# A list scheduler's costs and the pieces of a transposed softmax, in a hybrid decoder layer on one core

## The chip, the cores and the metric

The kernel runs on one core of a Trainium2 chip. The metric is device time in microseconds (us) of one execution. A core has five engines with queues of their own: TensorE (PE in the profile; its weight loads are PEld), VectorE (DVE), ScalarE (ACT), GpSimd (POOL) and SyncE (SP), which issues nearly all DMA transfers here. Each engine runs its instructions in the order of the program; semaphores hold an instruction until what it depends on is done. SBUF is the working memory, PSUM the one that matmuls write, in banks of 512 float32 values for each of 128 partitions.

## What is computed

One layer with 512 tokens and a model width of 1,024. A wide input projection feeds four causal mixers of width 512, each is gated, projected and merged, and an output projection is added to the input:

```python
xn = rms_norm(x, norm_g); z = xn @ w_in              # (512, 10528) columns, split
y_a = fox_attention(rms_norm(qa), rms_norm(ka), va, fa + b_forget)   # A: 8 heads
y_b = rg_lru(xb, ...)                                # B: recurrence
y_c = nsa_attention(rms_norm(qc), ...)               # C: 8 heads, three attentions
y_d = spatial_gating(ud, vd, ...)                    # D: gated MLP
ys = [y_a * silu(ga), y_b * silu(gb), y_c * silu(gc), y_d * silu(gd)]
proj = einsum('bsnw,nwd->bsnd', ys, w_branch)
out = x + sum_n(sigmoid(mg_n) * proj_n) @ w_out
```

What matters for the change is the causal softmax attention over 512 keys: once for each of the 8 heads of A, and twice for each of the 8 heads of C (called `s` and `w` in the kernel), so 24 times:

```python
s = q_i @ k.T * scale + bias                         # block i of 128 queries
p = masked_softmax(s, pos_k <= t)                    # rows are queries
o = p @ v                                            # needs p with keys on partitions
```

## The kernel before

**Precision.** Each float32 operand is split into a high part (a copy rounded to the matmul's type) and a low part (the difference): a copy on ACT or POOL, then a subtraction on DVE. A dense product takes three matmuls, high by high, high by low and low by high, each of 128 x 128 weights by 512 columns.

**Attention.** `scores` computes the four blocks of 128 queries of one unit (a head of A, or `s` or `w` of a head of C): two matmuls a block into a bank of pool `s`, mask and maximum on DVE, exponential on ACT into `p`, and normalisation on POOL. Because the mask is causal, `p` holds ten blocks of 128 x 128. `finish` transposes them on TensorE into PSUM (`transposes`, L734), so that keys lie on partitions: ACT copies the high part `ph` out and DVE subtracts it to make the low part `pl`. `values` multiplies both by the values into bank `o`. The ten blocks form three groups (keys 0; keys 1 and 3; keys 2), as `GROUPS` lists. They are transposed in five pieces of two blocks (`PIECES`), each into half a bank: `thalf` (L270) deals out the halves in turn. While A runs there is one such bank, `tb0`; for C there is a second, `tb1`, and `thalf` alternates between the two banks before it takes their other halves. Both have `tb` as their name in the profile.

**Filler.** Between these steps `fill(gap)` advances a queue of dense projections (`z_kv`, `z_qc`, `z_vd`, `z_ga`, `z_gd`, `z_ud`, `z_xb`, `z_gc` and others), so that TensorE has matmuls while it waits for the softmax.

**Order.** From the first projection to the end of attention the program doesn't issue directly: `Order` records each operation and, when a stack of pools is closed (`settle`), plans all that is pending. `plan` is a list scheduler. It keeps for each engine a time at which it is free, takes the engine that can start first, and of its operations that are ready the one that was recorded first. `cost` gives two numbers per operation: how long the engine is taken and when the result is there. `WAKE` is added between a result and an operation of another engine that needs it: 0.036 us for ACT, 0.033 for DVE, 0.064 for SP, 0.2 for POOL and 1.2 for PE. What the planner assumes sets the order only; on the chip, semaphores hold what isn't ready. Its tables know nothing of two engines that hinder each other. Behind attention, from the branches' merge on, the program issues in the order in which it is written.

**The start of C.** After the last head of A, DVE computes reciprocal roots (`tsc`), POOL multiplies keys and queries by them (`zkm`, `zq_c`), TensorE transposes these (`kt_s`, `qt_c`), ACT and DVE make operands of them (`ka_s`, `kb_s`, `q_c`), and the scores `s_s` follow. `sl` is a chain of small operations on DVE for branch B, `w_gd` and `w_w1k` are weights being split, `th_ga` and `y_a` belong to A's gate, `tblk` and `tblv` to C's compressed keys and values.

Of the kernel before, what the change touches and what calls it, by code (L numbers as in the profile page):

```python
# [11 lines left out]
F32R = mybir.dt.float32r  # L12
# [50 lines left out]
def f32(ap):  # L63
    return ap.bitcast(F32)


class Order:


    WAKE = {"ACT": 0.036, "DVE": 0.033, "SP": 0.064, "POOL": 0.2, "PE": 1.2}  # L70

    def __init__(self, nc):
        self.eng = {"ACT": nc.scalar, "DVE": nc.vector, "POOL": nc.gpsimd, "PE": nc.tensor, "SP": nc.sync}
        self.on, self.ops, self.seen, self.ring, self.before, self.stacks = False, [], {}, {}, {}, {}
        self.free = dict.fromkeys(self.eng, 0.0)
        self.wire, self.end, self.pending, self.queued = 0.0, {}, [], None

    def pool(self, real, stack):
        p = _Pool(self, real)
        self.stacks.setdefault(id(stack), []).append(p)  # L80
        return p

# [13 lines left out]
    def add(self, name, method, args, kw):  # L96
        aps = [(n == 0, a) for n, a in enumerate(args)] + [(k in ("out", "accum_out"), a) for k, a in kw.items()]
        aps = [(w, a) for w, a in aps if isinstance(a, bass.AP)]
        n, need = len(self.ops), {}
        boxes = [(w, *self.area(a)) for w, a in aps]  # L100
        for w, t, *box in boxes:
            if w and t in self.before:
                need.update((m, True) for m, *_ in self.seen.get(self.before[t], ()))
            for m, w2, b in self.seen.get(t, ()):
                if (w or w2) and box[0] < b[1] and b[0] < box[1] and box[2] < b[3] and b[2] < box[3]:
                    need[m] = need.get(m, False) or not (name == "PE" == self.ops[m][0] and w and w2)
        if self.queued is not None and self.ops[self.queued][0] == name:
# [3 lines left out]
        self.ops.append((name, method, args, kw, need, self.cost(name, kw, aps), {b[1] for b in boxes}))  # L111
        self.pending.append(n)
        return n

    @staticmethod
    def cost(name, kw, aps):

        free = max(a.free_size() for _, a in aps)
        scalar = any(not w and x.free_size() == 1 for w, x in aps)
        if name == "PE":  # L120
# [12 lines left out]
    def plan(self):  # L133

        ops, left, then, ready = self.ops, {}, {}, {}
        soon, able = {e: [] for e in self.eng}, {e: [] for e in self.eng}
        free, wire, end, out = dict(self.free), self.wire, self.end, []
        for i in self.pending:
            name, need = ops[i][0], ops[i][4]
            ready[i], left[i] = 0.0, 0  # L140
            for m, whole in need.items():
                if m in end:
                    ready[i] = max(ready[i], end[m] + self.WAKE[name] if whole else 0.0)
# [5 lines left out]
        done = {}  # L149
        for _ in self.pending:  # L150
            best = None
            for e in self.eng:
                t = free[e]
# [15 lines left out]
            out.append((i, t, free[e], wire, done[i]))  # L169
            for j in then.get(i, ()):  # L170
                f = ops[j][0]
                ready[j] = max(ready[j], done[i] + self.WAKE[f] if ops[j][4][i] else t)
# [5 lines left out]
    def settle(self, stack=None):  # L178
# [7 lines left out]
        for i, t, free, wire, done in out:  # L186
            name, method, args, kw, *_ = self.ops[i]
            getattr(self.eng[name], method)(*args, **kw)  # L188
            self.free[name], self.wire, self.end[i] = free, wire, done
        gone = {o[0] for o in out}  # L190
        self.pending = [i for i in self.pending if i not in gone]

# [10 lines left out]


class _Pool:
    def __init__(self, order, real):
        self.order, self.real, self.names, self.lines = order, real, [], {}

    def tile(self, *args, tag=None, bufs=None, **kw):
        if tag is not None:  # L210
            kw.update(tag=tag, bufs=bufs)
        t = self.real.tile(*args, **kw)
        self.names.append(t.tensor.name)
        if tag is not None:
            line = self.lines.setdefault(tag, [])
            if len(line) >= bufs:
# [6 lines left out]
def tile_hybrid_layer(ctx: ExitStack, tc: tile.TileContext, x, xT, units, small, bsp, out):  # L223
# [484 lines left out]
    def scores(u, gap):  # L708
# [25 lines left out]
    def transposes(u, n):  # L734
# [22 lines left out]
    def finish(u, gaps):  # L757
# [14 lines left out]
        fill(gaps[3])  # L772
# [969 lines left out]
```

## Time and profile before

| | before |
|---|---|
| median of 3 runs | 725.02 us (724.39 to 725.21) |
| the profiled execution, its own time | 724.89 us |
| its span, first to last instruction | 723.2 us |
| instructions in it | 9,672 |
| TensorE's granted clock, mean | 0.997 |
| bytes read from HBM, written | 65.64 MB, 2.10 MB |

The profile's page gives each engine's busy time, the span in 40 slices, the DMA queues, the chain of work that ended last, and the costliest groups of instructions. Its busy time of TensorE counts a matmul until its modelled end, so that two matmuls in a row overlap in it. DMA is light behind the first slices; its busy share in tenths, slice by slice:

```
DMA  8613222112112521200011223235432242143302
```

In the rows of the waits, an engine's idle time is put down to what ended it: engine, tile, "<-", engine and tile that released it, then the total in us, how many times, and the longest. In rows of the timeline the first number is the start in us from the span's start, the second the duration.

### The profile page before, as it was taken

Reading aid. Unit: us, or ns where it says so; the run is one execution under the profiler, and the core shown is the slowest. Engines: PE = TensorE matmul, PEld = TensorE weight load, DVE = VectorE, ACT = ScalarE, POOL = GpSimd, SP = SyncE. Lnnn points to the kernel's source line nnn. Section 1 sums busy time; section 2 is a strip of 40 time slices with the busy share of each in tenths; the row PEclk is TensorE's granted clock in tenths of the full one; section 3 lists DMA queues with packets and bytes.
Section 4 is the critical chain, followed back from the end, with each engine's and each line's share of the span. In section 5 each row is a group of like instructions: output and inputs, shape, how many; then the busy total and the mean of one; then the engine's idle time right before and its main releaser. Section 6 shows DMA issues by size and latency. Waiting matters only on the chain.

```text
span 723.2 us, 9672 instructions
## 1 busy us (share of the span) xinstructions
PE 703.2 (97%) x3357; PEld 574.4 (79%) x3357; DVE 575.8 (80%) x1138; ACT 367.2 (51%) x725; POOL 167.7 (23%) x230
## 2 busy tenths in 40 slices
PE   8999999999998999989999999999999999999997
PEld 6888788777866888878887787888888888888876
DVE  6797866666489838888997979999868858958995
ACT  4452565664523336766665891434443551554641
POOL 4115552442445312323343322100000000000000
PEclk9999999999999999999999999999999999999999
DMA  8613222112112521200011223235432242143302
GB/s 321 239 43 116 76 89 70 59 59 76 42 59 88 175 90 57 88 30 30 30 59 43 76 87 102 88 109 182 145 118 88 85 138 98 36 139 117 116 30 87
DMA packets 20640, 68.35 MB, mean 95 GB/s; under 512 B 2416, under 2 KB 2800, under 8 KB 20592
## 3 DMA queue, kind: packets, MB, share of 16 engines
q1 hardware_dynamic: 20160, 67.25, 27.9%
q8 instruction: 26, 0.43, 0.2%
q10 hardware_dynamic: 432, 0.49, 0.2%
q14 instruction: 22, 0.18, 0.1%
HBM read 65.64 MB, written 2.10 MB: 94 GB/s over the span
## 4 chain that ended last, share of the span: by engine, by line
PE 75%; DVE 14%; ACT 8%; issue 2%; DMA 1%; POOL 0%; DVEq 0%; SPq 0%; ACTq 0%
PE pj L201 10%; PE tb L188 4%; PE z_ud L188 3%; PE z_qc L188 3%; PE z_ka L188 3%; PE z_gb L201 3%; PE z_qa L188 3%; PE z_va L188 3%; PE z_mg L201 3%; PE z_xb L188 3%; PE mg2y L201 2%; PE z_kv L188 2%; PE z_vd L188 2%; PE mg3y L201 2%; PE mg1y L201 2%; PE z_gd L188 2%
## 5 line engine op out<-in xcount | busy, mean ns | idle before, releaser
L201 PE MATMUL pj<-w_wb,yh 128*128 128x512 f32 x256 | 80.2, 390 | 0.0
L201 PEld LDWEIGHTS pj<-w_wb,yh 128*128 128x128 f32 x256 | 48.1, 188 | 10.4 <-ACT tm L201 0.4
L201 PE MATMUL pj<-w_wb,yl 128*128 128x512 f32 x128 | 49.8, 389 | 0.0
L188 DVE TENSOR_TENSOR pl_a<-tb,ph_a 128x256 fp32r<-128x256 f32 x40 | 16.1, 421 | 18.7 <-PE tb L188 8.0
L201 DVE TENSOR_TENSOR w_wb<-r_wb,w_wb 128x512 fp32r<-128x512 f32 x32 | 21.8, 713 | 9.5 <-ACT w_wb L201 8.5
L201 PEld LDWEIGHTS pj<-w_wb,yl 128*128 128x128 f32 x128 | 24.0, 188 | 4.9
L188 ACT CAST ph_a<-tb 128x256 fp32r<-128x256 f32 x40 | 14.2, 375 | 25.6 <-PE tb L188 21.9
L188 ACT ACTIVATE p_s<-p_s,nm_s 128x512 f32<-128x512 f32 (+3 forms) x32 | 17.9, 562 | 12.9 <-DVE nm_s L188 12.7
L188 PE MATMUL z_gd<-xh,w_gd 128*128 128x512 f32 x64 | 23.6, 415 | 0.5 <-DVE sgd L188 0.5
L188 POOL TENSOR_SCALAR p_w<-p_w,nm_w 128x128 f32<-128x128 f32 (+3 forms) x32 | 16.9, 546 | 27.1 <-DVE nm_w L188 27.1
L188 POOL TENSOR_SCALAR p_s<-p_s,nm_s 128x128 f32<-128x128 f32 (+3 forms) x32 | 17.2, 556 | 25.3 <-ACT ph_w L188 10.8
L188 DVE CUSTOM_DVE_ANT_0 p_a<-s_a,maskm 128x512 f32<-128x512 f32 (+3 forms) x32 | 15.5, 488 | 9.3 <-PE s_a L188 8.1
L188 PE MATMUL z_xb<-xh,w_xb 128*128 128x512 f32 x64 | 22.9, 415 | 0.0
L188 PE MATMUL z_ud<-xh,w_ud 128*128 128x512 f32 x64 | 22.7, 402 | 0.0
L188 ACT ACTIVATE p_a<-p_a,nm_a 128x512 f32<-128x512 f32 (+3 forms) x32 | 17.9, 561 | 9.4 <-DVE nm_a L188 9.1
L188 PE MATMUL z_ga<-xh,w_ga 128*128 128x512 f32 x64 | 22.0, 404 | 0.0
L188 POOL TENSOR_SCALAR p_a<-p_a,nm_a 128x128 f32<-128x128 f32 (+3 forms) x32 | 18.6, 598 | 14.8 <-DVE nm_a L188 14.8
L188 ACT ACTIVATE p_w<-p_w,nm_w 128x512 f32<-128x512 f32 (+3 forms) x32 | 18.0, 564 | 7.3 <-DVE nm_w L188 6.2
L201 PE MATMUL z_gb<-xh,w_gb 128*128 128x512 f32 x64 | 21.1, 391 | 0.0
L201 ACT CAST w_wb<-r_wb 128x1024 fp32r<-128x1024 f32 x12 | 12.6, 1048 | 15.5 <-issue 15.5
L188 DVE TENSOR_TENSOR pl_s<-tb,ph_s 128x256 fp32r<-128x256 f32 x40 | 16.0, 415 | 4.9 <-ACT ph_s L188 4.6
L188 ACT CAST ph_w<-tb 128x256 fp32r<-128x256 f32 x40 | 13.9, 369 | 11.3 <-PE tb L188 8.9
(812 smaller groups left out, 2336.1 us busy)
## 6 DMA issues: line engine op xcount, KB each, us to landing
r_wb<-in_units_dram SPq DMA_DIRECT2D x16, 512.0 KB, 3.8
xt<-in_x_dram SPq DMA_DIRECT2D x4, 512.0 KB, 8.8
r_ga<-in_units_dram SPq DMA_DIRECT2D x4, 512.0 KB, 3.6
r_gd<-in_units_dram SPq DMA_DIRECT2D x4, 512.0 KB, 3.8
r_ud<-in_units_dram SPq DMA_DIRECT2D x4, 512.0 KB, 4.4
r_gc<-in_units_dram SPq DMA_DIRECT2D x4, 512.0 KB, 3.7
r_xb<-in_units_dram SPq DMA_DIRECT2D x4, 512.0 KB, 3.6
r_gb<-in_units_dram SPq DMA_DIRECT2D x4, 512.0 KB, 3.6
```

The source lines that it names most:

```text
L188: getattr(self.eng[name], method)(*args, **kw)
L201: return lambda *args, **kw: real(*args, **kw).ins
```

## The change

**Pieces.** The ten blocks are transposed in three pieces, one for each group, of four, four and two blocks; a piece has a bank to itself, and the banks are dealt out in turn. `transposes` issues four (or two) transposes, one copy on ACT and one subtraction on DVE of 512 (or 256) columns. `finish` calls the three pieces with `fill` and `values` between them in another order.

**The planner.** Its costs are new for every engine. A matmul now has a weight load that runs ahead of it and a time for its columns. PE's allowance of 1.2 us becomes 0.05 in `WAKE` plus 0.5 in `MARGIN` for results of other engines; POOL's becomes 0.11. Two exclusions are new. An operation that touches a PSUM tile is put off until the engine that touched that tile last is done with it, if that was another engine (`bank`). And operations of DVE (with a wide operand that isn't in PSUM) and of POOL that are marked so don't overlap: the later one starts when the other is done (`shared`).

```diff
-    WAKE = {"ACT": 0.036, "DVE": 0.033, "SP": 0.064, "POOL": 0.2, "PE": 1.2}
+    WAKE = {"ACT": 0.036, "DVE": 0.033, "SP": 0.064, "POOL": 0.11, "PE": 0.05}
+    MARGIN = {"ACT": 0.0, "DVE": 0.0, "SP": 0.0, "POOL": 0.0, "PE": 0.5}
...
         if name == "PE":
-            return max(0.112, free / 2400 + 0.018), free / 2400 + 0.175
+            weights = kw["lhsT"] if "lhsT" in kw else wide[0]
+            return aps[0][1].free_size() / 2400, 0.112 * max(64, min(128, weights.free_size())) / 128
         if name == "SP":
-            return 0.37, aps[0][1].partition_size() * free * 4 / 330e3
+            return 0.37, aps[0][1].partition_size() * aps[0][1].free_size() * 4 / 350e3
         if name == "DVE":
-            t, over = 0.17 + free / 850 + 0.06 * scalar, 0.08
-        elif name == "ACT":
-            t, over = 0.15 + free / 1140 + 0.09 * scalar + 0.12 * ("accum_out" in kw), 0.09
-        else:
-            two = sum(not w and x.free_size() == free for w, x in aps) > 1
-            t, over = (0.3 + free / 430 if two else 0.2 + free / 1100 + 0.1 * scalar), 0.02
-        return t - over, t
+            alone = bool(wide) and method not in ("tensor_reduce", "reciprocal", "memset") and not any(
+                x.tensor.name in self.psum for x in wide)
+            return 0.155 + free / 960 + 0.05 * scalar + 0.06 * (method == "tensor_tensor_scan" and free / 100), alone
+        if name == "ACT":
+            return 0.15 + free / 1140 + 0.09 * scalar + 0.15 * ("accum_out" in kw), False
+        if method == "memset":
+            return 0.1 + free / 1200, False
+        return (0.09 + free / 540 if len(wide) > 1 and method == "tensor_tensor" else 0.18 + free / 1170), True
...
             i = heapq.heappop(able[e])
-            busy, whole = ops[i][5]
-            free[e] = t + busy
-            if e == "SP":
-                wire = max(wire, t + 1.6) + whole
-                done[i] = wire + 0.6
+            open_ = max((bank[x][1] + self.WAKE[e] for x in ops[i][7] if x in bank and bank[x][0] != e), default=0.0)
+            if open_ > t:
+                heapq.heappush(soon[e], (open_, i))
+                continue
+            a, b = ops[i][5]
+            if e == "PE":
+                start = max(t + b, load)
+                load, free[e], done[i] = start + a + 0.014, start + max(a - 0.098, 0.003), start + a + 0.172
+            elif e == "SP":
+                wire = max(wire, t + 1.3) + b
+                free[e], done[i] = t + a, wire + 0.86
             else:
-                done[i] = t + whole
+                done[i] = t + a
+                if b:
+                    if shared[1] != e and shared[0] > t + 0.06:
+                        done[i] = shared[0] - 0.06 + a
+                    shared = done[i], e
+                free[e] = done[i] - self.OVER[e]
+            for x in ops[i][7]:
+                bank[x] = e, done[i]
...
-    PIECES = ((0, ((0, 0), (0, 1))), (0, ((0, 2), (0, 3))), (1, ((1, 1), (1, 2))), (1, ((1, 3), (3, 3))),
-              (2, ((2, 2), (2, 3))))
+    PIECES = (((0, 0), (0, 1), (0, 2), (0, 3)), ((1, 1), (1, 2), (1, 3), (3, 3)), ((2, 2), (2, 3)))
...
-        g_, blocks = PIECES[n]
-        t_ = thalf()
-        for c, (j, i) in enumerate(blocks):
+        ps_["ti"] = (ps_["ti"] + 1) % len(ps_["tb"])
+        n = P * len(PIECES[g_])
+        t_ = ps_["tb"][ps_["ti"]][:, 0:n]
+        for c, (j, i) in enumerate(PIECES[g_]):
             PE.transpose(t_[:, c * P:(c + 1) * P], u.p[:, OFF[i] + j * P:OFF[i] + (j + 1) * P], identf)
...
-        ACT.copy(ph[:, c:c + 256], t_)
-        DVE.tensor_tensor(pl_[:, c:c + 256], t_, f32(ph[:, c:c + 256]), op=ALU.subtract)
+        ACT.copy(ph[:, 0:n], t_)
+        DVE.tensor_tensor(pl_[:, 0:n], t_, f32(ph[:, 0:n]), op=ALU.subtract)
...
         transposes(u, 0)
+        fill(gaps[0])
         transposes(u, 1)
-        fill(gaps[0])
+        values(u, o, 0)
+        fill(gaps[1])
         transposes(u, 2)
-        values(u, o, 0)
-        transposes(u, 3)
-        fill(gaps[1])
-        transposes(u, 4)
         fill(gaps[2])
         values(u, o, 1)
```

The planner's answer moves instructions on every engine. Two places show how.

**TensorE, in the second head of A** (unit `a1`, tile `p_a_762`): `tb_79` is the bank `tb0`, `z_qc` are dense matmuls, `o_a` the values. Before, with four transposes nine matmuls ahead of the first row:

```order
L188 MATMUL o_a_800<-ph_a_801,v_a 128x512
L188 MATMUL tb_79<-identf,p_a_762 128x128 x2
L188 MATMUL z_qc_791<-w_qc.01_797,xh 128x512
L188 MATMUL o_a_800<-pl_a_802,v_a 128x512
L188 MATMUL tb_79<-identf,p_a_762 128x128 x2
L188 MATMUL z_qc_791<-w_qc.01_797,xl 128x512
L188 MATMUL z_qc_791<-w_qc.01_797,xh 128x512 x2
L188 MATMUL z_qc_791<-w_qc.01_797,xl 128x512
L188 MATMUL z_qc_791<-w_qc.01_797,xh 128x512
L188 MATMUL z_qc_792<-w_qc.01_797,xh 128x512
L188 MATMUL z_qc_792<-w_qc.01_797,xl 128x512
L188 MATMUL tb_79<-identf,p_a_762 128x128 x2
```

and now, at the same place:

```order
L211 MATMUL tb_79<-identf,p_a_762 128x128 x4
L211 MATMUL o_a_800<-pl_a_802,v_a 128x512
L211 MATMUL z_qc_791<-w_qc.01_797,xh 128x512
L211 MATMUL z_qc_791<-w_qc.01_797,xl 128x512
L211 MATMUL z_qc_791<-w_qc.01_797,xh 128x512 x2
L211 MATMUL z_qc_791<-w_qc.01_797,xl 128x512
L211 MATMUL z_qc_791<-w_qc.01_797,xh 128x512
L211 MATMUL o_a_800<-ph_a_803,v_a 128x384
L211 MATMUL z_qc_792<-w_qc.01_797,xh 128x512
L211 MATMUL z_qc_792<-w_qc.01_797,xl 128x512
L211 MATMUL tb_79<-identf,p_a_762 128x128 x2
```

Two matmuls stood between the second and the third visit to the bank, and seven between the third and the last; now there is one visit less, and ten matmuls stand between the last two.

**DVE, at the start of C**: before, from the second `sl` operation behind the split of `w_w1k` to the operand `kb_s`, behind which `q_c` follows at once:

```order
L188 TENSOR_SCALAR sl<-sl 128x4
L188 TENSOR_TENSOR sl<-sl 128x4
L188 TENSOR_SCALAR sl<-sl 128x4
L188 RECIPROCAL sl<-sl 128x4
L188 TENSOR_TENSOR sl<-sl 128x4 x2
L188 TENSOR_SCALAR sl<-sl 128x4
L188 SCALAR_TENSOR_TENSOR sl<-sl 128x4 x2
L188 SCALAR_TENSOR_TENSOR th_ga_1984<-th_ga_1984,z_ga_1971 128x512
L188 SCALAR_TENSOR_TENSOR sl<-sl 128x4
L188 TENSOR_TENSOR y_a<-y_a,th_ga_1984 128x512
L188 TENSOR_TENSOR w_gd_1994<-r_gd_1993,w_gd_1994 128x512
L188 SCALAR_TENSOR_TENSOR kb_s<-kt_s,cc,ka_s 64x512 x2
```

and now, from the split of `w_w1k` on:

```order
L211 TENSOR_TENSOR w_w1k_1950<-r_w1k_1949,w_w1k_1950 128x1024
L211 SCALAR_TENSOR_TENSOR th_ga_1952<-th_ga_1952,z_ga_1939 128x512
L211 TENSOR_TENSOR sl<-sl 128x4
L211 TENSOR_TENSOR y_a<-y_a,th_ga_1952 128x512
L211 TENSOR_TENSOR w_gd_1962<-r_gd_1961,w_gd_1962 128x512 x2
L211 SCALAR_TENSOR_TENSOR kb_s<-kt_s,cc,ka_s 64x512 x2
L211 SCALAR_TENSOR_TENSOR q_c_1936<-qt_c_1935,cc,q_c_1936 64x512 x2
```

All but one of the `sl` operations stand behind the scores now, and one half of `w_gd` more stands ahead of `kb_s`.

More of the change, by code (lines that the diff above doesn't have):

```diff
@@ L75, in __init__, with pool @@
         self.free = dict.fromkeys(self.eng, 0.0)
-        self.wire, self.end, self.pending, self.queued = 0.0, {}, [], None
-    def pool(self, real, stack):
-        p = _Pool(self, real)
+        self.wire, self.shared, self.load, self.psum, self.bank = 0.0, (0.0, None), 0.0, set(), {}
+        self.end, self.pending, self.queued = {}, [], None
+    def pool(self, real, stack, psum):
+        p = _Pool(self, real, psum)
         self.stacks.setdefault(id(stack), []).append(p)
@@ L110, in add, with cost @@
             self.seen.setdefault(t, []).append((n, w, box))
-        self.ops.append((name, method, args, kw, need, self.cost(name, kw, aps), {b[1] for b in boxes}))
+        self.ops.append((name, method, args, kw, need, self.cost(name, method, kw, aps), {b[1] for b in boxes},
+                         {b[1] for b in boxes} & self.psum))
         self.pending.append(n)
         return n
-    @staticmethod
-    def cost(name, kw, aps):
+    def cost(self, name, method, kw, aps):
         free = max(a.free_size() for _, a in aps)
         scalar = any(not w and x.free_size() == 1 for w, x in aps)
+        wide = [x for w, x in aps if not w and x.free_size() > 1]
         if name == "PE":
-            return max(0.112, free / 2400 + 0.018), free / 2400 + 0.175
+            weights = kw["lhsT"] if "lhsT" in kw else wide[0]
+            return aps[0][1].free_size() / 2400, 0.112 * max(64, min(128, weights.free_size())) / 128
         if name == "SP":
-            return 0.37, aps[0][1].partition_size() * free * 4 / 330e3
+            return 0.37, aps[0][1].partition_size() * aps[0][1].free_size() * 4 / 350e3
         if name == "DVE":
-            t, over = 0.17 + free / 850 + 0.06 * scalar, 0.08
-        elif name == "ACT":
-            t, over = 0.15 + free / 1140 + 0.09 * scalar + 0.12 * ("accum_out" in kw), 0.09
-        else:
-            two = sum(not w and x.free_size() == free for w, x in aps) > 1
-            t, over = (0.3 + free / 430 if two else 0.2 + free / 1100 + 0.1 * scalar), 0.02
-        return t - over, t
+            alone = bool(wide) and method not in ("tensor_reduce", "reciprocal", "memset") and not any(
[6 more added lines that the diff above has]
+        return (0.09 + free / 540 if len(wide) > 1 and method == "tensor_tensor" else 0.18 + free / 1170), True
+    OVER = {"ACT": 0.098, "DVE": 0.082, "POOL": 0.028}
     def plan(self):
@@ L136, in plan @@
         soon, able = {e: [] for e in self.eng}, {e: [] for e in self.eng}
-        free, wire, end, out = dict(self.free), self.wire, self.end, []
+        free, end, out = dict(self.free), self.end, []
+        wire, shared, load, bank = self.wire, self.shared, self.load, dict(self.bank)
+        margin = lambda e, m: self.WAKE[e] + (self.MARGIN[e] if ops[m][0] not in (e, "SP") else 0.0)
         for i in self.pending:
@@ L142, in plan @@
                 if m in end:
-                    ready[i] = max(ready[i], end[m] + self.WAKE[name] if whole else 0.0)
+                    ready[i] = max(ready[i], end[m] + margin(name, m) if whole else 0.0)
                 else:
@@ L148, in plan @@
                 heapq.heappush(soon[name], (ready[i], i))
-        done = {}
-        for _ in self.pending:
+        done, todo = {}, len(self.pending)
+        while len(out) < todo:
             best = None
@@ L161, in plan @@
             i = heapq.heappop(able[e])
[L162 to L169 removed]
+            open_ = max((bank[x][1] + self.WAKE[e] for x in ops[i][7] if x in bank and bank[x][0] != e), default=0.0)
[9 more added lines that the diff above has]
+                free[e], done[i] = t + a, wire + 0.86
+            else:
+                done[i] = t + a
[6 more added lines that the diff above has]
+                bank[x] = e, done[i]
+            out.append((i, dict(free), wire, shared, load, done[i]))
             for j in then.get(i, ()):
                 f = ops[j][0]
[L172 removed]
+                ready[j] = max(ready[j], done[i] + margin(f, i) if ops[j][4][i] else t)
                 left[j] -= 1
@@ L185, in settle @@
             out = out[:max((k + 1 for k, o in enumerate(out) if self.ops[o[0]][6] & names), default=0)]
-        for i, t, free, wire, done in out:
+        for i, self.free, self.wire, self.shared, self.load, self.end[i] in out:
             name, method, args, kw, *_ = self.ops[i]
+            self.bank.update((x, (name, self.end[i])) for x in self.ops[i][7])
             getattr(self.eng[name], method)(*args, **kw)
-            self.free[name], self.wire, self.end[i] = free, wire, done
         gone = {o[0] for o in out}
@@ L213, in tile @@
         self.names.append(t.tensor.name)
+        if self.psum:
+            self.order.psum.add(t.tensor.name)
         if tag is not None:
@@ L228, in pool @@
     def pool(name, stack=ctx, **kw):
-        return order.pool(stack.enter_context(tc.tile_pool(name=name, bufs=1, reuse_waits="tile", **kw)), stack)
+        return order.pool(stack.enter_context(tc.tile_pool(name=name, bufs=1, reuse_waits="tile", **kw)), stack,
+                          kw.get("space") is PSUM)
     def behind(op):
```

14 lines of the change are left out of this document (6 added, 8 removed).

## The prediction

> **What bounds the kernel now.** The page's first part gives each engine's busy time, the fourth the chain of work that ended last; one row of that chain in order of time shows TensorE undisturbed.
>
> ```profile
> PE 703.2 (97%) x3357; PEld 574.4 (79%) x3357; DVE 575.8 (80%) x1138; ACT 367.2 (51%) x725; POOL 167.7 (23%) x230
> PE 75%; DVE 14%; ACT 8%; issue 2%; DMA 1%; POOL 0%; DVEq 0%; SPq 0%; ACTq 0%
> 523.68 5.44 PE mg2z L201 x24
> ```
>
> TensorE carries 75% of the chain, and its undisturbed pace is 5.44 / 24 = 0.227 us for a matmul of 512 columns. The change adds and removes no matmul, so it can only win or lose time in which TensorE does not issue. Busy time by stage (length, then TensorE's busy time; DVE's is the fourth number) shows where that is:
>
> ```profile
> 75.00:200.00 125.00, 121.46 (x606) 97.87 (x606) 83.13 (x186) 73.95 (x171) 51.86 (x80) 1.00 0.21 68
> 200.00:275.00 75.00, 70.18 (x332) 56.34 (x331) 56.98 (x126) 23.30 (x51) 26.68 (x29) 0.98 0.33 106
> 275.00:400.00 125.00, 120.64 (x685) 99.95 (x683) 107.96 (x328) 83.94 (x239) 45.45 (x74) 1.00 0.15 47
> 400.00:723.20 323.20, 318.07 (x1430) 261.26 (x1429) 271.23 (x398) 153.94 (x211) 17.27 (x13) 1.00 0.31 102
> ```
>
> The planner orders what lies before about 395 us: first the eight heads of branch A, then the start of branch C, then its sixteen heads. TensorE is not busy for 3.5, 4.8 and 4.4 us there, 12.7 in all. That is a lower bound, since records are longer than the pace. The waits between 75 and 400 us say for what (total, times, longest), of the weight loads first and then of the matmuls:
>
> ```profile
> PEld tb L188 <- ACT ph_a L188: 4.1, 8, 0.9
> ...
> PEld tb L188 <- DVE pl_a L188: 3.1, 5, 0.7
> PEld tb L188 <- ACT ph_s L188: 2.9, 6, 0.7
> ...
> PEld tb L188 <- DVE pl_s L188: 2.1, 3, 1.5
> PEld tb L188 <- ACT ph_w L188: 1.8, 5, 0.5
> ```
>
> ```profile
> PE s_s L188 <- DVE q_c L188: 2.9, 1, 2.9
> PE tb L188 <- DVE pl_a L188: 1.9, 4, 0.5
> PE tb L188 <- ACT ph_s L188: 1.1, 3, 0.4
> ...
> PE tb L188 <- DVE pl_s L188: 1.0, 1, 1.0
> PE tb L188 <- ACT pc L188: 0.8, 1, 0.8
> ...
> PE tb L188 <- ACT ph_a L188: 0.5, 1, 0.5
> ...
> PE tb L188 <- ACT ph_w L188: 0.4, 2, 0.2
> ```
>
> Two things stand out: the bank `tb` into which probabilities are transposed (14.0 us by the weight loads, 5.7 us by the matmuls), and one wait of 2.9 us.
>
> **Part 1, whole banks.** One head of branch A, in order of time:
>
> ```profile
> 115.98 0.38 PE L188 MATMUL tb<-identf,p_a 128*128 128x128 f32 x2
> ...
> 116.42 0.40 PE L188 MATMUL o_a<-pl_a,v_a 128*128 128x512 f32 x1
> 116.44 0.37 ACT L188 CAST ph_a<-tb 128x256 fp32r<-128x256 f32 x1 [1.72 <-PE tb L188]
> ...
> 116.86 0.14 PEld L188 LDWEIGHTS tb<-identf,p_a 128*128 128x128 f32 x1 [0.47 <-ACT ph_a L188]
> ...
> 117.23 0.42 DVE L188 TENSOR_TENSOR pl_a<-tb,ph_a 128x256 fp32r<-128x256 f32 x1 [1.72 <-PE tb L188]
> 117.71 0.14 PEld L188 LDWEIGHTS tb<-identf,p_a 128*128 128x128 f32 x1 [0.71 <-DVE pl_a L188]
> 117.71 0.33 PE L188 MATMUL tb<-identf,p_a 128*128 128x128 f32 x1 [0.52 <-DVE pl_a L188]
> ...
> 117.79 0.48 PE L188 MATMUL z_qc<-w_qc.01_797,xl 128*128 128x512 f32 x1
> ```
>
> The pair at 115.98 fills one half of the bank, the pair at 116.86 the other. Yet the second pair starts only after ACT's copy of the first half (116.81), DVE's subtraction only after that transpose, and the last transpose only after DVE (117.65): three engines take turns on one bank, whichever half they touch. A transpose takes 0.11 us (115.98 to 116.42 hold two and one matmul of `z_qc`, 0.227). So the matmul of 117.79 was due at 116.42 + 0.227 + 0.22 = 116.87: 0.92 us lost, where the weight loads' rows show 0.47 + 0.71 = 1.18. With that ratio of 0.78 the 14.0 us cost 10.9 us; the matmuls' rows give 5.7. I take 10.9, because the timeline prices it like that.
>
> What replaces it? Ordered rows times these durations give TensorE's other work between the last transpose of a piece and the first of the next in the same bank. Before, 0.45 us once in each of the eight heads of branch A, and under 1 us at some 25 of 79 places in branch C. Now 2.22 us or more at all 23 places of branch A, and in branch C 1.8 or more at 44 of 47. A full bank needs a transpose, ACT's copy of 512 columns and DVE's subtraction from PSUM; the nearest rows of that shape (minimum, median, maximum in ns) are
>
> ```profile
> L188 ACT ACTIVATE th_ga<-z_ga x4: 598/600/605, 198.4 to 219.9; 128x512 f32<-128x512 f32 x4
> L188 DVE SCALAR_TENSOR_TENSOR th_ga<-th_ga,z_ga x4: 672/678/682, 199.0 to 225.2; 128x512 f32<-128x512 f32 x4
> ```
>
> which make 0.33 + 0.60 + 0.68 and three gaps of 0.05 (116.81 to 116.86): 1.76 us, below 2.22. Before, a half needed 0.33 + 0.37 + 0.42 + 0.15 = 1.27 us, and where 1.59 us of work stood ahead of it, the head's last pair came on time, 0.23 us after the matmul ahead:
>
> ```profile
> 119.27 0.39 PE L188 MATMUL z_qc<-w_qc.01_797,xl 128*128 128x512 f32 x1
> 119.50 0.38 PE L188 MATMUL tb<-identf,p_a 128*128 128x128 f32 x2
> ```
>
> Three places of branch C stay short of 1.76, by 2.8 us together at most, and ACT or DVE will at times be at something else when the bank is handed over. I leave 0.125 us a head, 24 heads, 3.0 us (between 0 and the 10.9). **Part 1: 7.9 us less.** Five copies and five subtractions a head become three of each: 5 x 0.37 - (2 x 0.60 + 0.37) = 0.28 us less of ACT and 5 x 0.42 - (2 x 0.68 + 0.42) = 0.32 us less of DVE, 6.7 and 7.7 us over 24 heads. I count that as nothing: it lies beside TensorE's work. If DVE were the bound in branch C, up to 16 x 0.32 = 5.1 us of it would count.
>
> **Part 2, the start of branch C.** DVE, then TensorE:
>
> ```profile
> 220.95 0.57 DVE L188 TENSOR_TENSOR sl<-sl 128x4 f32<-128x4 f32 x1
> 221.55 0.98 DVE L188 TENSOR_SCALAR sl<-sl 128x4 f32<-128x4 f32 x1
> ...
> 227.18 1.51 DVE L188 SCALAR_TENSOR_TENSOR kb_s<-kt_s,cc,ka_s 64x512 fp32r<-64x512 f32 x2
> 228.72 1.53 DVE L188 SCALAR_TENSOR_TENSOR q_c<-qt_c,cc,q_c 64x512 fp32r<-64x512 f32 x2
> ```
>
> ```profile
> 226.36 0.39 PE L188 MATMUL z_gd<-xh,w_gd 128*128 128x512 f32 x1
> 229.60 0.47 PE L188 MATMUL s_s<-ka_s,q_c 128*128 128x512 f32 x1 [2.86 <-DVE q_c L188]
> ```
>
> Tiny operations on four columns, up to 0.98 us each while GpSimd works, stand ahead of `kb_s` and `q_c`, which the scores wait for. From 220.95 to 227.18 DVE spends 6.2 us; the new order keeps one `sl` (0.57), `th_ga` (0.68), `y_a` and two halves of `w_gd` (0.7 each, by the same width): 3.4 us, or about 4.7 if GpSimd stretches the last three. So the operands come 1.5 to 2.8 us sooner, and the ordered rows put 0.7 us more matmul work ahead of the scores: the wait of 229.60 - 226.36 - 0.23 = 3.0 us shrinks to 0 to 0.8; I take 0.4, a gain of 2.6. The wait has a sequel:
>
> ```profile
> 230.60:234.00 3.40, 3.40 (x11) 2.82 (x10) 3.37 (x8) 1.41 (x4) 1.04 (x1) 0.50 0.34 104
> ```
>
> For 3.4 us the granted clock is 0.50, which costs 1.7 us, and that goes with the wait. The Trainium skill, in "TensorE: Matmul & The Clock Gate", Part 1, says the clock drops after an idle window of about 3.4 us. By that rule a wait of 3.0 us would cost no clock, and the sum would be 1.7 us worse; the trace shows the drop behind this shorter wait, and the trace decides. Against it, `tblk` of 1,024 columns (estimated at 1.3 us, twice the row of 512) moves ahead of the last `tsc` step, for which GpSimd and the first transposes of this stage wait; but 1.6 us more matmuls stand ahead of these too. I charge 0.5. On the DMA queue two loads change place with the next one; the later of them,
>
> ```profile
> L188 SPq DMA_DIRECT2D r_w1v<-in_units_dram x2: 328/328/328, 231.6 to 237.1; - x2
> L188 ACT CAST w_w1v<-r_w1v x2: 1047/1048/1048, 240.3 to 255.5; 128x1024 fp32r<-128x1024 f32 x2
> ```
>
> is issued 8.7 us ahead of its first use, so one load more ahead of it costs nothing unless that lead is used up. **Part 2: 2.6 + 1.7 - 0.5 = 3.8 us less**, between 0 (GpSimd's chain holds the scores anyway) and 4.7.
>
> **Part 3, thinner margins.** The planner assumed 1.2 us between a result and a matmul that uses it, now 0.55. Work between a piece's last transpose and the first use of its copy was 1.0 us or more in 71 of 72 cases, now below that in five; a full copy needs 0.33 + 0.60 + 0.10 = 1.03. Five short by 0.2 to 0.4 make 1.5 us, late scores something more: **2.0 us lost**, between 0 and 14 (0.1 us at each of 72 `ph` and 72 `pl`).
>
> **Sum** against the profiled execution's own 724.89 us (span 723.2; the median of the runs is 725.02): 724.89 - 7.9 - 3.8 + 2.0 = **715.2 us**. Behind 400 us the same work follows, with 5.1 us not busy in 323; it starts earlier by as much.
>
> **Rivals.** (a) DVE becomes the bound in branch C: 107.96 of 125 us busy speaks for it, the 17 us idle there against. Then the part of `tb` in branch C, (2.9 + 2.1 + 1.8) x 0.78 = 5.3 us, stays: 720.5. (b) The wait of part 2 stays, because GpSimd's eight products set it: 719.0. (c) The change does not do what it says: bank waits turn into waits for `ph` and `pl`, the start stays: 724.9. (d) Slower: the thin margin costs 0.1 us at each of the 144 first uses, 14.4 instead of 2.0: 727.6; it decides from 11.7 / 144 = 0.08 us. Against it stands that the distances for `pl` mostly exceed 1.76. (e) All goes: `tb` 14.0, start 4.7, no loss: 706.2.
>
> **How the numbers follow.** Forecast 0.48, (a) 0.15, (b) 0.14, (c) 0.06, (d) 0.09, (e) 0.08. Faster by over 0.2% (about what a measurement here can tell from no change): all but (c) and (d), 0.85; within it (c), 0.06; slower (d), 0.09. The range 707 to 722.5 takes in the forecast, (a) and (b), and leaves out (c), (d) and most of (e).
>
> **What would show it.** Right: `tb` waits of weight loads below 4 us in place of 14; no clock of 0.50 behind 200 us; `s_s` waiting under 1 us. Wrong: waits of `o_a` and `o_s` for `ph` and `pl` of over 5 us (d); DVE above 95% busy in branch C (a); the wait of `s_s` as before (b).

## The result and the profile after

| | before | after |
|---|---|---|
| median of four runs | 724.92 us (724.39 to 725.21) | 713.08 us (712.27 to 713.58) |
| ratio | | 0.9836, 95% interval 0.9819 to 0.9853 |
| profiled execution, its own time | 724.89 us | 713.0 us |
| its span | 723.2 us | 711.3 us |

The kernel is 11.8 us faster. The page of the changed kernel, first part and chain of waits:

```profile
PE 700.0 (98%) x3357; PEld 573.4 (81%) x3357; DVE 571.0 (80%) x1090; ACT 362.3 (51%) x677; POOL 171.2 (24%) x230
PE 78%; DVE 13%; issue 3%; ACT 3%; DMA 2%; POOL 2%; SPq 0%; DVEq 0%; POOLq 0%; ACTq 0%
```

TensorE still sets the end; ACT's share of the chain fell from 8% to 3%. Busy time by stage, in the columns of before:

```profile
75.00:200.00 125.00, 123.46 (x627) 101.66 (x626) 85.72 (x173) 73.52 (x158) 56.01 (x82) 1.00 0.21 68
200.00:275.00 75.00, 73.13 (x359) 58.62 (x358) 60.19 (x146) 27.16 (x62) 28.61 (x33) 1.00 0.35 113
275.00:400.00 125.00, 123.88 (x690) 102.39 (x689) 110.09 (x290) 86.69 (x215) 45.84 (x70) 1.00 0.14 47
```

TensorE is not busy for 1.5, 1.9 and 1.1 us in place of 3.5, 4.8 and 4.4, and the clock is 1.00 where it was 0.98. DVE is busy for 110.09 of 125 us in branch C, 88%, and is not the bound. The waits between 75 and 400 us, of the weight loads and then of the matmuls:

```profile
PEld tb L211 <- DVE pl_a L211: 2.2, 4, 1.0
...
PEld tb L211 <- POOL p_s L211: 1.4, 3, 0.8
...
PEld o_s L211 <- ACT ph_w L211: 0.8, 3, 0.3
PEld o_s L211 <- DVE pl_s L211: 0.8, 3, 0.4
...
PEld o_s L211 <- DVE pl_w L211: 0.6, 2, 0.3
...
PEld o_s L211 <- ACT ph_s L211: 0.4, 1, 0.4
...
PEld o_a L211 <- DVE pl_a L211: 0.3, 1, 0.3
```

```profile
PE z_gd L211 <- DVE w_gd L211: 0.8, 1, 0.8
PE s_s L211 <- DVE q_c L211: 0.7, 1, 0.7
PE tb L211 <- DVE pl_a L211: 0.6, 1, 0.6
PE z_kv L211 <- DVE v_a L211: 0.5, 1, 0.5
PE tb L211 <- POOL p_s L211: 0.5, 2, 0.3
PE z_kv L211 <- DVE w_kv.00_743 L211: 0.3, 1, 0.3
PE tb L211 <- DVE pc L211: 0.2, 1, 0.2
PE s_w L211 <- DVE nm_w L211: 0.2, 1, 0.2
PE z_gd L211 <- DVE sgd L211: 0.2, 1, 0.2
PE g L223 <- DVE xcl L223: 0.2, 1, 0.2
```

Of the 14.0 us for which the bank `tb` waited for `ph` and `pl`, 2.2 are left. The second view has one more thing to read: the first uses of `ph` and `pl` (`o_s`, `o_a`) make the weight loads wait 2.9 us in all, and no matmul among its rows waits for them. A weight load runs beside the matmul ahead of it, so part of such a wait is hidden, but not all: paired in order with their matmuls, the ten loads that wait 2.9 us have matmuls that start 1.1 us late in all, 0.01 to 0.34 us each; before, four such loads waited 1.75 us and cost 0.85. One bank in branch A, in order of time:

```profile
114.28 0.60 PE L211 MATMUL tb<-identf,p_a 128*128 128x128 f32 x4
...
114.93 0.59 ACT L211 CAST ph_a<-tb 128x512 fp32r<-128x512 f32 x1
...
115.55 0.69 DVE L211 TENSOR_TENSOR pl_a<-tb,ph_a 128x512 fp32r<-128x512 f32 x1 [0.43 <-ACT ph_a L211]
...
117.02 0.60 PE L211 MATMUL tb<-identf,p_a 128*128 128x128 f32 x4
```

The last of the four transposes starts at 114.28 + 3 x 0.11 = 114.61, and DVE is done with the bank at 116.24: 1.63 us, where the prediction had put 1.76. The bank is needed again at 117.02, so nobody waits.

To price waits in TensorE's own time, I take the start of each of the 3357 matmuls less the start of the one ahead and less the latter's pace (columns / 2400 + 0.014 us, at least 0.11), and put what is left down to the later matmul; what a matmul loses at a granted clock of 0.50 counts in it too. For 73 to 400 us, in us, with the two kernels of the first experiments and two later ones beside them:

| kernel | `tb` in A | `tb` in C | other, 73 to 400 | elsewhere | sum | span |
|---|---|---|---|---|---|---|
| before | 5.1 | 9.7 | 12.7 | 7.4 | 34.9 | 723.2 |
| whole banks, old planner | 0.3 | 7.8 | 13.8 | 7.8 | 29.7 | 717.9 |
| half banks, new planner | 2.3 | 5.5 | 10.0 | 7.1 | 24.9 | 713.1 |
| after | 1.3 | 3.8 | 11.0 | 7.0 | 23.1 | 711.3 |
| half banks, new planner, no bank rule | 8.0 | 12.9 | 12.1 | 8.4 | 41.4 | 729.6 |
| after, no bank rule | 0.7 | 6.2 | 15.8 | 6.6 | 29.3 | 717.5 |

The sums differ as the spans do (before to after 11.8 and 11.9). From before to after `tb` gives 9.7; the start of branch C (the scores `s_s`, `kt_s`, `qt_c` and `z_gd`) falls from 7.7 to 3.5, which gives 4.2; 2.1 come back net in small pieces, such as `z_xb` 1.0, `s_w` 0.9, `g` 0.8 and `z_gc` 0.7.

### The profile page after: what moved, and what is told of

Read it like the earlier page. It is cut to its first block, busy times and chain, and to the rows that moved or that the text cites. A ratio compares the mean times of both kernels' runs of the same rounds, so it can differ in the third digit from the quotient of the medians.

```text
span 711.3 us, 9561 instructions
## 1 busy us (share of the span) xinstructions
PE 700.0 (98%) x3357; PEld 573.4 (81%) x3357; DVE 571.0 (80%) x1090; ACT 362.3 (51%) x677; POOL 171.2 (24%) x230
## 4 chain that ended last, share of the span: by engine, by line
PE 78%; DVE 13%; issue 3%; ACT 3%; DMA 2%; POOL 2%; SPq 0%; DVEq 0%; POOLq 0%; ACTq 0%
PE pj L223 9%; PE z_mg L223 6%; PE tb L211 3%; PE z_qc L211 3%; PE z_ud L211 3%; PE z_gb L223 3%; PE z_qa L211 3%; PE z_va L211 3%; PE o_s L211 3%; PE mg2y L223 2%; PE z_vd L211 2%; PE mg1y L223 2%; PE z_xb L211 2%; PE z_ka L211 2%; PE z_kv L211 2%
## 5 line engine op out<-in xcount | busy, mean ns | idle before, releaser
L211 DVE TENSOR_TENSOR pl_a<-tb,ph_a 128x512 fp32r<-128x512 f32 (+1 forms) x24 | 14.4, 598 | 14.2 <-ACT ph_a L211 14.0
L211 ACT CAST ph_a<-tb 128x512 fp32r<-128x512 f32 (+1 forms) x24 | 12.4, 517 | 23.3 <-PE tb L211 23.1
L211 ACT ACTIVATE p_s<-p_s,nm_s 128x512 f32<-128x512 f32 (+3 forms) x32 | 17.8, 559 | 11.8 <-DVE nm_s L211 11.1
L211 POOL TENSOR_SCALAR p_a<-p_a,nm_a 128x128 f32<-128x128 f32 (+3 forms) x32 | 19.7, 633 | 12.7 <-DVE nm_a L211 12.0
L211 DVE CUSTOM_DVE_ANT_0 p_s<-s_s,maskm 128x512 f32<-128x512 f32 (+3 forms) x32 | 15.0, 485 | 4.3 <-PE s_s L211 3.8
L211 DVE TENSOR_TENSOR pl_w<-tb,ph_w 128x512 fp32r<-128x512 f32 (+1 forms) x24 | 14.0, 598 | 3.0 <-ACT ph_w L211 2.8
```

## The experiments

Every kernel was timed beside the kernel before on its chip, which took 724.9 to 725.3 us each time. The theory: whole banks remove the handovers, the new order the wait at the start of branch C, and thin margins give a little back. The first rival: the planner's new rules do it all, whatever the pieces.

**1. Whole banks alone.** The planner of before with the new pieces, and with `transposes`, `values` and `finish` as the change has them.

```diff
-    PIECES = ((0, ((0, 0), (0, 1))), (0, ((0, 2), (0, 3))), (1, ((1, 1), (1, 2))), (1, ((1, 3), (3, 3))),
-              (2, ((2, 2), (2, 3))))
+    PIECES = (((0, 0), (0, 1), (0, 2), (0, 3)), ((1, 1), (1, 2), (1, 3), (3, 3)), ((2, 2), (2, 3)))
```

> The planner of before, costs and all, with the whole-bank pieces of after: part 1 alone. Theory (the handovers of the bank are the main gain, whoever plans): the waits of transposes for ph and pl shrink as in the changed kernel, 8 to 10 us less, 715 to 717 us; the start of branch C stays as before, with thirteen sl operations ahead of kb_s, s_s waiting about 3 us and a clock of 0.50 behind it. Rival (the pieces gain only where the new planner spaces them): 722 us or more, tb waits of the weight loads above 8 us. Rival (the pieces are the whole change): 713 us.

Measured: 719.69 us (719.04 to 723.59, six runs), ratio 0.9931, interval 0.9914 to 0.9948: some 5 us less, half of what the theory wanted. Its transposes by group of probabilities (busy, mean ns, then the idle time ahead and what ended it), weight loads:

```profile
L188 PEld LDWEIGHTS tb<-identf,p_a 128*128 128x128 f32 x80 | 10.1, 140 | 2.9 <-DVE pl_a L188 0.2
L188 PEld LDWEIGHTS tb<-identf,p_s 128*128 128x128 f32 x80 | 10.1, 140 | 4.1 <-DVE pl_w L188 1.7 <-DVE pl_s L188 0.3 <-issue 0.3
L188 PEld LDWEIGHTS tb<-identf,p_w 128*128 128x128 f32 x80 | 9.9, 140 | 7.3 <-DVE pc L188 3.9 <-POOL p_w L188 1.4 <-ACT pc L188 0.2
```

In branch A the handovers are gone. In branch C 7.8 of 9.7 us stay: of the weight loads' waits 3.9 us (3.2 us of late matmul starts) are for `pc`, the compressed probabilities, which pass through the same banks and of which I had taken no account, and 1.7 for the last subtraction of another head. The pieces became fewer, but the planner does not know when a bank is given back.

**2. The new planner alone**, with the five half-bank pieces: the changed kernel with the lines of the diff above turned back, `transposes`, `values` and `finish` with them.

> The planner of after with the five half-bank pieces of before: parts 2 and 3 alone. Theory: the start of branch C gains about 4 us, thin margins lose about 2, the tb waits stay near 14 us: 722 to 724 us. Rival (the planner's knowledge of banks brings the gain, the size of the pieces none): 713 to 717 us, and tb waits below 7 us. Rival (thin margins cost more than the start gains, as in the prediction's slower case): above 726 us.

Measured: 715.13 us (714.80 to 716.51, four runs), ratio 0.9863, interval 0.9850 to 0.9875. The rival is right here: nearly all of the gain is had without whole banks. One head of branch A in this kernel:

```profile
113.72 0.60 PE L211 MATMUL tb<-identf,p_a 128*128 128x128 f32 x4
...
116.25 0.38 PE L211 MATMUL tb<-identf,p_a 128*128 128x128 f32 x2
116.38 0.48 PE L211 MATMUL o_a<-pl_a,v_a 128*128 128x512 f32 x1
116.70 0.38 PE L211 MATMUL tb<-identf,p_a 128*128 128x128 f32 x2
...
118.95 0.38 PE L211 MATMUL tb<-identf,p_a 128*128 128x128 f32 x2
```

```profile
117.17 0.65 ACT L211 CAST ph_a<-tb 128x256 fp32r<-128x256 f32 x2 [2.16 <-PE tb L211]
```

Two halves are filled back to back, as they were before, and 2.2 us are left to the readers; the next two halves stand 0.45 us apart, and ACT copies both together when they are full, where before its copy stood between them. In this head the planner, told that a bank is closed to other engines, thus builds whole banks out of half ones by itself. So the two parts of the change cure one stall: alone they take 6.7 and 7.0 us off `tb`, together 9.7.

**3. The start of branch C alone.** The kernel before, with one line.

```diff
         if name == "c0":
-            next(gl)
+            with behind(last["dve"]):
+                next(gl)
```

> The kernel before, with the sl chain tied behind the first eviction of branch C, so that none of its operations stands ahead of kb_s and q_c: the start of branch C alone, without any new cost or margin. Theory (the sl operations on DVE hold the scores): s_s waits under 1 us in place of 2.9, no clock of 0.50 behind 200 us, 3.5 to 4.5 us less, 720.4 to 721.4 us. Rival (GpSimd's products or the transposes hold the scores anyway): the wait moves to another operand and the time stays within 1 us of 724.9. If the clock drops although the wait is short, the gain is 2.6 and not 4.3.

Measured: 720.94 us (720.78 to 721.92, five runs), ratio 0.9942, interval 0.9930 to 0.9954, mean clock 1.000 in all five. The theory holds, with its size: 4.3 us. In the view of the weight loads `s_s` keeps 0.5 us of wait ("issue").

**4. Without the rule that DVE and GpSimd exclude each other.**

```diff
-                    if shared[1] != e and shared[0] > t + 0.06:
+                    if False:
```

> The changed kernel without the rule that DVE and GpSimd exclude each other in the planner; pieces, banks and margins as after. In its order sixteen sl operations stand ahead of kb_s again, after has one. Theory (this rule alone moves the sl operations, and their place is worth about 4 us): 716 to 717.5 us, s_s waits 2 us or more, perhaps with a clock of 0.50 behind it. Rival (the start is held by something else, the rule has no effect): 713 us within 1.

Measured: 722.36 us (722.08 to 722.52, five runs), ratio 0.9958, interval 0.9945 to 0.9971. The mechanism is the expected one, but the loss of 9.3 us against after is twice the 4 that I had put down for it. Up to 3.4 us of it are the clock: it stood at 0.50 for 3.41 us twice (from 214.79 and from 228.45 us), and the mean was 0.992 to 0.998 in all five runs. DVE, GpSimd and TensorE in this kernel:

```profile
211.06 1.22 DVE L211 TENSOR_TENSOR tblv<-trs,tblv 128x1024 fp32r<-128x1024 f32 x1
212.20 1.28 DVE L211 TENSOR_TENSOR w_gd<-r_gd,w_gd 128x512 fp32r<-128x512 f32 x2
...
216.98 1.00 DVE L211 TENSOR_TENSOR sl<-sl 128x4 f32<-128x4 f32 x1
218.02 0.54 DVE L211 TENSOR_SCALAR sl<-sl 128x4 f32<-128x4 f32 x1
...
222.37 1.95 DVE L211 SCALAR_TENSOR_TENSOR sl<-sl 128x4 f32<-128x4 f32 x7
...
224.84 1.51 DVE L211 SCALAR_TENSOR_TENSOR kb_s<-kt_s,cc,ka_s 64x512 fp32r<-64x512 f32 x2
```

```profile
211.30 2.66 POOL L211 TENSOR_TENSOR zkm<-zkm,tsc 128x256 f32<-128x256 f32 x1 [4.81 <-DVE tsc L211]
...
217.93 0.61 POOL L211 TENSOR_TENSOR zkm<-zkm,tsc 128x256 f32<-128x256 f32 x1
```

```profile
214.01 0.33 PE L211 MATMUL kt_s<-identf,zkm 128*128 128x128 f32 x1 [2.56 <-POOL zkm L211]
...
227.27 0.47 PE L211 MATMUL s_s<-ka_s,q_c 128*128 128x512 f32 x1 [1.75 <-DVE q_c L211]
242.43 0.74 PE L211 MATMUL hpsk<-w_w1k,tblk 128*128 128x256 f32 x4 [2.07 <-DVE w_w1k L211]
```

The same product on GpSimd takes 0.61 us beside DVE's four-column operations and 2.66 us beside `tblv` and `w_gd`, each of which reads two wide operands from SBUF (211.06 to 213.48). A planner that reckons with 0.56 (0.09 + 256 / 540) sends TensorE to `kt_s` too early, which is some 2 of the 2.56 us. `hpsk` waits 2.07 us for a weight of which GpSimd's part came late; that this goes back to the same error is not shown. The rule thus serves at more than the one place that the prediction saw.

**5 and 6. Without the bank rule**, once with the half-bank pieces, once with the whole ones.

```diff
-            open_ = max((bank[x][1] + self.WAKE[e] for x in ops[i][7] if x in bank and bank[x][0] != e), default=0.0)
+            open_ = max((bank[x][1] + self.WAKE[e] for x in ops[i][7] if False), default=0.0)
```

> The planner of after with the half-bank pieces (715.1 us in the second experiment, transposes' waits down to 7.6 us of stall from 14.7), but without its rule that a PSUM bank is closed to other engines while one of them uses it. Theory (this rule spaces the half-bank pieces: it is a second cure of the same stall, which is why the two gains overlap): tb waits of the weight loads for ph and pl back above 10 us, 719 to 722 us. Rival (the shorter margin and the new costs of TensorE space them): 714 to 716 us, waits as in the second experiment.

> The changed kernel, whole-bank pieces and all, without the bank rule of the planner alone. Theory (whole banks leave the rule little to do, since the distances between pieces hardly change): 712.5 to 714.5 us. Rival (the rule matters for the banks of scores and projections too): 716 us or more, and waits for s_w, s_s or z banks grow.

Measured: with half banks 731.10 us (730.74 to 731.35, four runs), ratio 1.0090, interval 1.0077 to 1.0103; with whole banks 720.80 us (719.24 to 721.87, six runs), ratio 0.9945, interval 0.9932 to 0.9957. The theory of the fifth holds in kind and falls short in size: the rule is worth 16 us there, and the kernel is slower than before (13.1 us of it are `tb`, and one stretch of 3.41 us at a clock of 0.50, from 84.28 us, falls on a wait of 2.4 us ahead of `z_kv`). Its weight loads:

```profile
L211 PEld LDWEIGHTS tb<-identf,p_w 128*128 128x128 f32 x80 | 9.5, 140 | 9.1 <-DVE pl_w L211 2.9 <-ACT ph_w L211 2.8 <-issue 1.9
L211 PEld LDWEIGHTS tb<-identf,p_a 128*128 128x128 f32 x80 | 9.5, 140 | 13.4 <-DVE pl_a L211 6.8 <-ACT ph_a L211 5.0
```

The theory of the sixth falls and its rival's figure comes: with whole banks the rule is still worth 7.7 us. Some 1.5 us of that are the clock, whose mean was 0.995 to 0.998 in four of the six runs (720.75 to 721.87 us) and 1.000 in the others (719.24 and 719.79), the profiled one among them. Of the 6.2 us of its span, 1.8 are `tb`, 2.5 the `o_s` matmuls and 2.0 `z_kv`; the new wait of 2.4 us ahead of `z_kv` shows how the rule helps elsewhere. DVE and TensorE without it, and then with it (after):

```profile
81.85 1.51 DVE L211 SCALAR_TENSOR_TENSOR kb_a<-kt_a,cc,ka_a 64x512 fp32r<-64x512 f32 x2 [0.51 <-ACT ka_a L211]
83.40 1.06 DVE L211 TENSOR_TENSOR w_kv.00_743<-r_kv.00_742,w_kv.00_743 128x512 fp32r<-128x512 f32 x1
```

```profile
84.51 0.73 PE L211 MATMUL z_kv<-w_kv.00_743,xh 128*128 128x512 f32 x2 [2.37 <-DVE w_kv.00_743 L211]
```

```profile
81.61 1.11 DVE L211 TENSOR_TENSOR w_kv.00_743<-r_kv.00_742,w_kv.00_743 128x512 fp32r<-128x512 f32 x1
82.64 1.50 DVE L211 SCALAR_TENSOR_TENSOR kb_a<-kt_a,cc,ka_a 64x512 fp32r<-64x512 f32 x2
```

`kb_a` reads the bank `kt_a`, which ACT is still reading. Without the rule DVE takes it up first, waits 0.51 us, and the weights for which TensorE waits stand behind it for two operations; with the rule DVE does the weights meanwhile.

**7. Whole banks and the start of branch C**, in the planner of before: the diffs of the first and the third experiment together.

> The planner of before with the whole-bank pieces, and the sl chain tied behind the first eviction of branch C: parts 1 and 2 of the prediction without any new cost or margin. Theory (the two do not overlap, since they lie at different places): 719.7 - 4.3 = 715.4 us, between 714.8 and 716.2; no clock below 1.00. Rival (the new start meets the waits for pc that the first experiment shows in branch C): 717 us or more.

Measured: 715.10 us (714.77 to 715.82, four runs), ratio 0.9870, interval 0.9858 to 0.9883: 719.69 - 4.6. These two do add, and together they reach, without any new cost or rule, what the new planner reaches with half banks (715.13).

**8 to 11. The margin.** In the changed kernel 1.2, 0.35 and 0.05 us in place of 0.55; and 1.2 in the kernel of the fifth experiment, which has no bank rule. Each is this line with its number (1.15, 0.3, 0.0):

```diff
-    MARGIN = {"ACT": 0.0, "DVE": 0.0, "SP": 0.0, "POOL": 0.0, "PE": 0.5}
+    MARGIN = {"ACT": 0.0, "DVE": 0.0, "SP": 0.0, "POOL": 0.0, "PE": 1.15}
```

> The changed kernel with the margin ahead of TensorE back at 1.2 us in all (0.55 in after), nothing else. Theory of the prediction's part 3 (thin margins cost 2 us): 710.5 to 711.5 us. Rival (the margin costs nothing here, first uses of ph and pl wait 3 us in both): 712.5 to 713.5. Rival (a longer margin starves TensorE of ready work): 714 us or more.

> The planner of after with the half-bank pieces, without its bank rule (731.1 us) and with the margin ahead of TensorE back at 1.2 us. Theory (the long margin stood in for the bank rule: it spaced transposes from whatever went before, and so the prediction's loss by thin margins is real, but only where no rule knows the banks): some 10 us less, 719 to 722 us, which is the kernel before less the 4.3 us of the start. Rival (the loss in that experiment has nothing to do with the margin): 730 to 732 us.

> The changed kernel with a margin of 0.05 us ahead of TensorE in place of 0.55. Theory (with the bank rule a margin only guards the first uses of ph and pl; their distances in the order now fall short of 1.03 and 1.7 us by 7.7 us in all, against 4.0 in after): 2 to 4 us more, 715 to 717 us, the o_a and o_s waits for ph and pl above 5 us. Rival (shorter is better all the way, from 715.0 at 1.2 over 713.1 at 0.55): 711 to 712.5.

> The changed kernel with a margin of 0.35 us ahead of TensorE in place of 0.55. The distances in the order fall short by 2.3 us in all, against 4.0 in after. Theory (the first uses decide): 711.5 to 713 us. Rival (there is no slope at this place, orders differ by chance): anything from 712 to 715.

**12. After, with `sl` behind the first eviction**, the diff of the third experiment.

> The changed kernel with the sl chain tied behind the first eviction of branch C, as in the third experiment. Only one sl operation stands ahead of kb_s in after. Theory (part 2 is all gained already): within 1 us of 713. Rival (the chain still costs where it lies now, between the operands of the windowed heads): 711 to 712 us.

| kernel | us (range, runs) | ratio to before, interval |
|---|---|---|
| after, margin 1.2 | 715.04 (714.35 to 716.39, 4) | 0.9870, 0.9854 to 0.9886 |
| after, margin 0.55 | 713.08 (712.27 to 713.58, 4) | 0.9836, 0.9819 to 0.9853 |
| after, margin 0.35 | 714.59 (714.51 to 715.45, 4) | 0.9859, 0.9843 to 0.9874 |
| after, margin 0.05 | 715.79 (715.36 to 715.98, 4) | 0.9872, 0.9857 to 0.9886 |
| after, `sl` later | 715.27 (714.58 to 716.12, 4) | 0.9866, 0.9849 to 0.9883 |
| half banks, no bank rule, margin 1.2 | 726.76 (724.61 to 727.79, 10) | 1.0026, 1.0015 to 1.0037 |

The margin of 1.2 is not faster, so the loss of 2.0 that the prediction charged is not there. The time is that of the third forecast (714 or more), but that TensorE lacked ready work is not shown. With 0.05 the theory's time came (715 to 717) but not its sign: the weight loads of the first uses of `ph` and `pl` wait 4.2 us, not above 5. With 0.35 the theory missed and only the rival's wide range holds; with `sl` later both forecasts missed. Nor is there a slope to be read: each of these four small edits of the changed kernel, the harmless one of `sl` too, gave 1.5 to 2.7 us more, and the waits that grew lie in part at places that the edit never meant. With `sl` later, DVE waits for GpSimd's part of a weight, `pc` stands behind that, and TensorE waits for `pc`:

```profile
334.02 0.69 DVE L223 TENSOR_TENSOR w_gc<-r_gc,w_gc 128x512 fp32r<-128x512 f32 x1 [0.94 <-POOL w_gc L223]
334.74 0.42 DVE L211 TENSOR_TENSOR pc<-tb,pc 64x256 fp32r<-64x256 f32 x1
...
335.62 0.44 PE L211 MATMUL tb<-identf,p_w 128*128 128x128 f32 x2 [1.75 <-ACT pc L211]
```

Differences of this size say which order the planner happened upon, not what a rule is worth; whether 0.55 is better than its neighbours for a reason stays open, and so does whether some 2 of the 11.8 us are a lucky order rather than a rule. Without the bank rule the margin does count: 726.76 in place of 731.10, 4.3 us of the 10 that I expected, net all of it at `tb`. So the long margin of before stood in for the missing rule, in part; the wait of 2.4 us ahead of `z_kv` stays. The new costs were not tried alone. None of these kernels beats the changed one.

## Why the prediction was right, and where it was not

713.08 us lies within 707 to 722.5 and 2.1 below the forecast of 715.2; the likeliest case came, and what was to show it did (`tb` waits of 2.2 us for `ph` and `pl`, `s_s` 0.7, no clock of 0.50 behind 200 us).

**Part 1** said 7.9 us less; TensorE's own time says 9.7. Pairing each weight load with its matmul splits that, by the same reckoning to within 0.2 us:

| late starts of transposes, 73 to 400 us | before | after |
|---|---|---|
| loads that waited for `ph` and `pl` | 10.0 | 1.2 |
| loads whose wait is put down to "issue" | 2.1 | 0 |
| loads that waited for GpSimd's scaling or `pc` | 0.3 | 2.0 |
| transposes without such a wait | 2.6 | 2.2 |

What the prediction priced, it priced well: 10.9 by one head's ratio of 0.78, where all heads give 10.0 (0.70 of 14.3 us of load waits). What it left out were the six loads under "issue"; four of them start 0.12 us after DVE's last read of a bank for `pc`, so they are likely the same handover. What it left standing, 3.0 for late readers, was mis-sized and misplaced: 1.2 are left for `ph` and `pl`, and 2.0 come from GpSimd's scaling and `pc`, which were not in it. The estimated handover of 1.76 us was good (1.63), and the distances read from the new order were the right thing to read: they held what both parts of the change did. The name was wrong. "Whole banks" carry only 5 to 6 of the 11.8 us when they stand alone and 2.0 when they are added to the new planner, which is no more than small edits of the order gave (1.5 to 2.7); the bank rule makes them mostly superfluous. The prediction did not see that rule as a cause at all. Luck has a part in the sum: what it left out pulled both ways, 2.1 us of gain under "issue" and 1.7 us more for scaling and `pc`.

**Part 2** said 3.8 us less, 2.6 + 1.7 - 0.5. The third experiment gives 4.3 (interval 3.3 to 5.1), the accounting of after 4.2. Its cause is shown: tying the `sl` chain back removes wait and clock drop, and taking the exclusion rule away brings them back. The 1.7 us for the clock was a matter of odds: of the 35 runs of the kernel before that were timed beside the experiments, five had a mean clock of 1.000, and they took 723.3 to 724.0 us. The charge of 0.5 for `tblk` was not found; `kt_s` waits less after than before (0.3 against 1.7 us in TensorE's time).

**Part 3** failed: "Five short by 0.2 to 0.4 make 1.5 us". They are short, and ten loads wait 2.9 us there, but their matmuls are only 1.1 us late, against 0.85 before, and the time ahead of all `o` matmuls together does not grow. The 2.1 us that did come back are spread over projections and scores, so the sum was helped by a term whose place was wrong.

**The rivals.** (a) DVE as the bound: 88% busy, no. (b) GpSimd's products hold the start: no, the third experiment. (c) Waits move to `ph` and `pl`: no. (d) Thin margins slower by 0.1 us a use: not with the bank rule; without it the changed planner with half banks is in fact slower than before, by 6 us, though through the bank and not through first uses. (e) All of `tb` and all of the start: no, 5.1 us of `tb` and 3.5 us of the start are left.

## What to carry to other kernels

Where a planner orders the work, an exclusion that it does not know (a bank that one engine holds, a path that two engines share) is paid in the places where an in-order queue stands behind it, and teaching it the exclusion is one cure: here taking one of the two rules out again costs 7.7 or 9.3 us, the clock's part included. Removing the causes by hand is another: whole banks and one line for `sl` brought the planner of before to 715.10 us, the new planner with half banks came to 715.13 and with whole banks to 713.08, a difference as small as that between orders. Separate a change into its parts on the chip before naming the one that carries it, and read what an edit of a planner is worth against the 2 us or so by which each of four small edits moved this kernel. Price weight-load waits by the starts of the matmuls behind them.

## What the runs showed of the hardware

The clock's drop does not follow from the length of one wait. Before, `s_s` waited 2.86 us and 3.4 us at 0.50 followed; with whole banks alone (first experiment) the same matmul waits as long, and the clock stays:

```profile
225.38 0.47 PE L188 MATMUL s_s<-ka_s,q_c 128*128 128x512 f32 x1 [2.86 <-DVE q_c L188]
```

```profile
225.40:229.40 4.00, 4.00 (x21) 3.37 (x22) 3.94 (x9) 1.29 (x4) 1.04 (x1) 1.00 0.19 60
```

Of that kernel's six runs four had a mean clock of 1.000 and took 719.0 to 719.8 us, one 0.998 and 720.75, one 0.995 and 723.59. Without the exclusion rule (fourth experiment) a wait of 1.75 us was enough:

```profile
229.20:230.80 1.60, 1.60 (x6) 1.31 (x5) 1.60 (x6) 0.93 (x3) 0.00 (x0) 0.50 0.19 51
```

What it follows in these traces is how little TensorE did in a fixed window. The clock records of all 14 profiled runs change on a grid of 3.41 us, whose phase differs from run to run, and between 60 and 700 us each drop lasts one step of it. The share of the step ahead that matmuls fill (by pace, columns / 2400 us, at least 0.11):

| kernel | step, us | share | clock in the next step |
|---|---|---|---|
| half banks, no bank rule | 80.87 to 84.28 | 0.18 | 0.50 |
| no exclusion rule | 211.38 to 214.79 | 0.19 | 0.50 |
| before | 227.19 to 230.61 | 0.25 | 0.50 |
| after, margin 1.2 | 221.17 to 224.58 | 0.31 | 0.50 |
| half banks, no bank rule, margin 1.2 | 82.72 to 86.13 | 0.34 | 0.50 |
| no exclusion rule | 225.03 to 228.45 | 0.36 | 0.50 |
| whole banks, old planner | 220.34 to 223.75 | 0.54 | 1.00 |
| whole banks, old planner | 223.75 to 227.16 | 0.45 | 1.00 |

Every other step at full clock in these runs (some 2,600) has a share of 0.41 or more, and none is followed by a drop. So the wait of 2.86 us fell mostly into one step before and was spread over two with whole banks alone, and with margin 1.2 two waits of 0.67 and 0.77 us in one step, beside small matmuls, were enough. What the chip itself counts is not shown.

The Trainium skill, in "TensorE: Matmul & The Clock Gate", Part 1, has the clock set by activity in a window that runs freely, so that the phase decides and runs of one kernel differ; that agrees. The Trainium skill's idle window of about 3.4 us agrees in length with the 3.41 us here, but the window need not be idle: TensorE was at work for 0.18 to 0.36 of it.

And a tiny operation can be dear: `sl` on 4 columns took up to 1.00 us on DVE beside GpSimd's products (fourth experiment), while the 13 `sl` operations of the third experiment's kernel beside which GpSimd was idle took 0.14 to 0.16 us each.
